# DeltaNet joins and pair weights apart from the recurrent steps, through DRAM, and gate products between the steps, in a two-layer hybrid encoder

## The chip, the cores and the metric

The kernel runs on one core of a Trainium2 chip. The metric is the device time of one execution in microseconds; each kernel is run several times and the median counts. One further execution is taken with the hardware profiler, and every row shown here comes from it.

TensorE (PE in the profile) multiplies matrices, VectorE (DVE), ScalarE (ACT) and GpSimd (POOL) work on tiles, and SyncE (SP) issues nearly all transfers of the part that the change touches. Each engine takes its instructions in one fixed order and waits at the first that isn't ready. Before the kernel is built, a scheduler writes these orders down, from the order of the program and its own estimates.

## The reference, cut to what matters

```python
# layer 0; DeltaNet runs once forwards and once on the flipped sequence
a = where(strict, beta * (k @ k.T) * gam, 0)          # gam = exp(gc_i - gc_j)
tmat = a + eye
u = solve_triangular(tmat, beta * v)
w = solve_triangular(tmat, beta * exp(gc) * k)
attn = (q @ k.T) * gam
def step(state, ...):                                 # over chunks of 64
    v_new = u - w @ state
    o = (q * exp(gc)) @ state + attn @ v_new
    state = exp(gl) * state + (k * exp(gl - gc)).T @ v_new
...
mix = concat([sigmoid(mo) * head_rms(mlstm), head_rms(deltanet)]) * silu(z)
x = x + gate * (mix @ w_out)
```

There are 1024 tokens, 1024 features, four mLSTM heads and four DeltaNet heads. A second layer (convolution and windowed attention) follows; the change doesn't touch it.

## The kernel before

The program treats the sequence in `NCH` = 8 chunks of 128 tokens, so that a triangular inverse of 128 by 128 per chunk, head and direction stands for two of the reference's chunks. Products of large matrices are made in three passes of 512 columns each: high part times high part, high times low, low times high (`whi`, `wlo` for weights, `hhi`, `hlo` for the normed input). ACT makes the high part of a weight (L264) and POOL the low part (L265).

Layer 0 goes through these stages. Projections of q, k and v for DeltaNet and mLSTM go on in the order of a list of steps (L925). `dn_system` builds the triangular systems per chunk and stores them to `nd_d` and `nt_d`. `dn_inverse` inverts blocks of 32, then joins them to blocks of 64, stored to `xl_d`; its last stages use the tiles `iG`, `iV`, `iT`. `mlstm` runs eight steps in both directions at once (`S`, `num`, `Cps`). `dn_step(j)` then runs the DeltaNet recurrence: chunk j forwards and chunk 7-j backwards. Last come the gates (`gate_chunk`, `gate_pair`), the output product and the second layer.

A `dn_step` of one direction loads the two 64-blocks of the inverse into `Y` (L951), loads two more blocks into `aux` (L953, L954), multiplies them (`T1`), copies the result (L958), multiplies again (`T2`) and copies it into `Y` (L962). This is the join of two blocks of 64. If the chunk is visited for the first time, it makes the pair weights of both directions: `KQ` on PE, two broadcast loads of `gc_d` (L975), a triangular mask (POOL, L599), four exponentials (ACT, L624), a product (DVE, L977); the other direction's weights go to `at_d` (L979) and are loaded at the second visit (L967). Then follow, in both cases, `kS` (from step 1 on), `Yr`, `qS`, `dS` (state update) and `o`, with ACT and DVE work after each.

`gate_chunk(c)` loads a weight of 512 KB (`wraw`, L258), splits it, multiplies (`z`) and applies the gate activation (L758 to L760), for c below 4 also `mo` (L768, L769); the result goes to `mix_d`. `gate_pair(6)` does two at once. `mix0(t)` loads the gates of 128 tokens (L1091), normalizes, transposes (`nT`) and multiplies (L1100). `out0(t)` splits that (L1054 on ACT, L1055 on DVE) and makes the output product `y`. In the program, `gate_chunk(2)` to `gate_chunk(5)` and `gate_pair(6)` stand behind all eight steps, and the scheduler mixes them in among these: `gate_pair(6)` is tied to the end of step 3, `mix0(3)`, the output weight and the first three `out0` to the end of `gate_pair`.

While layer 0 runs, SP also carries the loads of the second layer's modulation weight (L439), one `U` tile at a time, each made free by POOL (L443).

Of the kernel before, what the change touches and what calls it, by code (L numbers as in the profile page):

```python
# [17 lines left out]
P = 128  # L18
# [38 lines left out]
def trunk(ctx, tc, x, c, norm_g, ada_w, ada_b, ev_w_in, ev_m_gate_b, ev_dn_dt_bias, ev_dn_a_log,  # L57
# [69 lines left out]
    def nm(s):  # L127
        uid[0] += 1
        return f"{s}_{uid[0]}"
# [430 lines left out]
    nc.sync.dma_start(out=gc_d, in_=cs1[96:104])  # L560
    nc.sync.dma_start(out=nmu_d, in_=nmu[0:8])
# [40 lines left out]
    def brow(src, d, ch):  # L602
        return src[4 * d:4 * d + 4, ch * P:(ch + 1) * P].rearrange("(o h) l -> o h l", o=1).to_broadcast([P, 4, P])
# [32 lines left out]
    def dn_system(ch):  # L636
# [5 lines left out]
        nc.sync.dma_start(out=B_, in_=gc_d[:, tcs].rearrange("(o r) l -> o r l", o=1).to_broadcast([P, 8, P]))  # L642
# [15 lines left out]
    def dn_inverse(n):  # L658
# [41 lines left out]
        zd_r = ring(4096, 2, 4, 4, 32)  # L700
        own = diag4.rearrange("p (o g i) -> p o g i", o=1, g=4).to_broadcast([P, 4, 4, 32])
        spread = lambda ap: ap.rearrange("p u (o i) -> p u o i", o=1).to_broadcast([P, 4, 4, 32])
        for ch in range(NCH):
            u4 = slice(4 * ch, 4 * ch + 4)
            ZD, GD = next(zd_r), next(zd_r)
            nc.vector.tensor_tensor(out=ZD, in0=spread(Z[:, u4, :]), in1=own, op=ALU.mult)
            ps = bank(nm("iG"), (P, 4, 32), "C")
            for h in range(4):
                mm(ps[:, h, :], ZD[:, h].rearrange("p g i -> p (g i)"), AT[:, 4 * ch + h, :], True, True)
            nc.vector.tensor_tensor(out=GD, in0=spread(ps), in1=own, op=ALU.mult)  # L710
            ps = bank(nm("iV"), (P, 4, 32), "C")
            for h in range(4):
                mm(ps[:, h, :], GD[:, h].rearrange("p g i -> p (g i)"), B[:, 4 * ch + h, :], True, True)
            nc.scalar.copy(out=Z[:, u4, :], in_=ps)
            ps = bank(nm("iT"), (P, 4, 32), "C")
            tr(ps.rearrange("p g j -> p (g j)"), Z[:, u4, :].rearrange("p h i -> p (h i)"))
            nc.scalar.copy(out=VT[:, :, ch, :], in_=ps)
        for d, b, g_ in lanes4:
            nc.sync.dma_start(out=part(xl_d[0], d, b, 0, 1), in_=Z[g_])
        for h in range(4):  # L720
            nc.sync.dma_start(out=xl_d[1][:, :, :, h, 32:64, 0:32].rearrange("d b c i j -> i (d b c) j"),
                              in_=VT[32 * h:32 * h + 32].rearrange("p g c j -> p (g c) j"))

# [201 lines left out]
    for step, n in ((dn_q, 0), (dn_v, 0), (m_q, 0), (dn_q, 1), (m_q, 1), (dn_q, 2), (dn_q, 3), (m_k, 1), (m_v, 0), (m_v, 2), (m_v, 3), (m_v, 1), (m_k, 0), (mlstm, 0), (dn_v, 1), (dn_inverse, 0), (gate_chunk, 0), (dn_v, 2), (gate_chunk, 1), (dn_v, 3)):  # L925
        step(n)
    Y_r, aux_r, ke_r, vv_r, v2_r = (ring(0, 2, 4, P), ring(1024, 2, 2, 4, 64), ring(2048, 2, 4, P), ring(3072, 3, 4, P),
                                    ring(5632, 2, 4, P))
# [9 lines left out]
    seen2 = set()  # L938

    def dn_step(j):  # L940
        for d in range(2):
# [14 lines left out]
            for h in range(4):  # L956
                mm(ps[sb, h, :], aux[fb, 1, h, :], aux[fb, 0, h, :], True, True)
            nc.scalar.copy(out=aux[sb, 0], in_=ps[sb])  # L958
            ps = bank(nm("T2"), (P, 4, 64), "C")
            for h in range(4):  # L960
                mm(ps[fb, h, :], aux[sb, 0, h, :], Y[sb, h, sb], True, True)
            nc.scalar.copy(out=Y[fb, :, sb], in_=ps[fb])  # L962


            if ch in seen2:
                B_ = etile(("E", "Em")[d])
                nc.sync.dma_start(out=B_, in_=at_d[d, ch])  # L967
            else:
                ps = bank(nm("KQ"), (P, 4, P), "t")
                for h in range(4):  # L970
                    mm(ps[:, h, :], kT[h][:, tcs], qT[h][:, tcs], True, True)
                Bs = {}
                for d_ in (d, 1 - d):
                    B_ = Bs[d_] = etile(("E", "Em")[d_])
                    nc.sync.dma_start(out=B_, in_=brow(gc_d, d_, ch))  # L975
                    decays(B_, d_, ch)
                    nc.vector.tensor_tensor(out=B_, in0=B_, in1=ps, op=ALU.mult)  # L977
                B_ = Bs[d]
                nc.sync.dma_start(out=at_d[1 - d, ch], in_=Bs[1 - d])  # L979
# [167 lines left out]
    marks = [dn_step(j) for j in range(NCH)]  # L1147
    G2 = (None,)*4
    for cidx, j in zip(range(2, 6), G2):
        with ExitStack() if j is None else tc.issue_after(marks[j]):  # L1150
            gate_chunk(cidx)

    with tc.issue_after(marks[3]):
        half_done = gate_pair(6)
# [451 lines left out]
```

## Time and profile before

| | us |
|---|---|
| runs of the kernel | 1512.96, 1513.93, 1521.6 |
| their median | 1513.93 |
| the profiled execution | 1522.57 |
| span of its trace | 1520.8 |
| PE busy in the span | 1344.9 (88%) |
| DVE, ACT, POOL busy | 879.0, 585.9, 460.4 |

The profiled execution is 8.64 us longer than the median, and its mean granted TensorE clock is 0.933 of full speed. DeltaNet's steps lie between 549 us (the last mLSTM step) and 776 us (the first output product). From 866 us on only the second layer is left.

### The profile page before, as it was taken

How to read it: one execution, taken by the hardware profiler on the slowest of the kernel's cores; microseconds unless marked ns; L12 is line 12 of the kernel's file. 1: busy time of each engine (PE TensorE's matmuls, PEld its weight loads, DVE VectorE, ACT ScalarE, POOL GpSimd, SP SyncE). 2: the span in 40 equal slices, each digit the busy share in tenths (PEclk: the TensorE clock that was granted, in tenths of full speed). 3: DMA queues.
4: the chain of work that ended last, by engine and by line, in shares of the span. 5: the costliest groups of instructions: out<-in, count | busy, mean ns of one | idle time of the engine just before them, and what ended most of it. 6: DMA issues, size and time to landing. Idle time of an engine off the chain costs nothing. (4 is left out here: it accounts for less than half of the span.)

```text
span 1520.8 us, 20504 instructions
## 1 busy us (share of the span) xinstructions
PE 1344.9 (88%) x7331; PEld 1070.9 (70%) x7331; DVE 879.0 (58%) x1622; ACT 585.9 (39%) x1415; POOL 460.4 (30%) x357
## 2 busy tenths in 40 slices
PE   3978958878878988988999989889999999998998
PEld 2766746657667866777878857667776767876786
DVE  6789456933324641345854539998886454336334
ACT  5354454454444323343443321123324743326212
POOL 3454523444234511210234102322125233022210
PEclk9898987989899999889999999999999998997899
DMA  9334479369667785455655271010241233245322
GB/s 319 102 83 113 106 168 235 109 223 177 177 180 229 234 203 147 124 140 143 211 189 156 84 144 56 28 56 22 67 140 43 66 127 119 84 143 158 102 82 104
DMA packets 256456, 205.11 MB, mean 135 GB/s; under 512 B 59391, under 2 KB 219667, under 8 KB 256227
## 3 DMA queue, kind: packets, MB, share of 16 engines
q1 hardware_dynamic: 235555, 193.32, 45.1%
q10 hardware_dynamic: 20800, 10.49, 2.4%
q8 instruction: 58, 0.95, 0.3%
q14 instruction: 43, 0.35, 0.1%
HBM read 148.45 MB, written 58.98 MB: 136 GB/s over the span
## 5 line engine op out<-in xcount | busy, mean ns | idle before, releaser
L265 POOL TENSOR_TENSOR wlo<-wraw,whi 128x1024 fp32r<-128x1024 f32 x60 | 163.2, 2720 | 358.6 <-ACT whi L264 345.9
L1245 DVE SCALAR_TENSOR_TENSOR u<-xp,U,u 128x1009 f32<-128x1009 f32 (+14 forms) x120 | 176.2, 1502 | 1.0
L264 ACT CAST whi<-wraw 128x1024 fp32r<-128x1024 f32 x60 | 62.6, 1044 | 136.5 <-PE gb L139 49.1
L139 PE MATMUL z<-hhi,whi 128*128 128x512 f32 x256 | 108.1, 422 | 4.5 <-ACT mo L768 4.2
L139 PE MATMUL z<-hlo,whi 128*128 128x512 f32 x256 | 106.8, 417 | 0.0
L139 PE MATMUL z<-hhi,wlo 128*128 128x512 f32 x256 | 106.3, 415 | 0.0
L443 POOL TENSOR_TENSOR U<-U 128x512 f32<-128x512 f32 x56 | 79.4, 1419 | 76.9 <-ACT U L441 74.4
L139 PE MATMUL y<-wohi,mhi 128*128 128x512 f32 x240 | 97.9, 409 | 2.2 <-ACT mhi L1054 2.1
L139 PE MATMUL y<-wolo,mhi 128*128 128x512 f32 x240 | 96.8, 403 | 0.0
L139 PE MATMUL y<-wohi,mlo 128*128 128x512 f32 x240 | 96.1, 402 | 0.4 <-DVE mlo L1055 0.3
L441 ACT ACTIVATE U<-U,cs 128x512 f32<-128x512 f32 x64 | 45.9, 722 | 84.8 <-DMA U<-in_ada_w_dram 83.5
L599 POOL TENSOR_SCALAR_AFFINE_SELECT E<-E 128x512 f32<-128x512 f32 x32 | 21.4, 670 | 170.3 <-DMA E<-gc_d 71.3
L1397 DVE COPY U<-pT 128x512 f32<-128x512 f32 x48 | 32.5, 689 | 55.7 <-PE pT L158 55.6
L139 PEld LDWEIGHTS z<-hhi,whi 128*128 128x128 f32 x256 | 50.7, 198 | 16.7 <-ACT mo L768 4.6
L139 PEld LDWEIGHTS z<-hhi,wlo 128*128 128x128 f32 x256 | 50.5, 197 | 11.9 <-issue 1.1
L139 PEld LDWEIGHTS z<-hlo,whi 128*128 128x128 f32 x256 | 50.6, 197 | 11.3 <-issue 0.9
L139 PEld LDWEIGHTS y<-wohi,mhi 128*128 128x128 f32 x240 | 46.0, 192 | 13.5 <-ACT mhi L1054 2.5
L139 PE MATMUL sc<-ak,aq 128*128 128x256 f32 (+1 forms) x128 | 44.2, 429 | 11.6 <-DVE o L1372 9.8
L139 PEld LDWEIGHTS y<-wohi,mlo 128*128 128x128 f32 x240 | 45.9, 191 | 11.9 <-DVE mlo L1055 1.3
L1370 DVE CUSTOM_DVE_ANT_0 pt<-sc,U 128x256 f32<-128x256 f32 (+1 forms) x64 | 25.9, 404 | 48.6 <-PE sc L139 23.4
L139 PEld LDWEIGHTS y<-wolo,mhi 128*128 128x128 f32 x240 | 46.2, 193 | 10.3
L1374 ACT ACTIVATE pt<-pt,o 128x256 f32<-128x256 f32 (+1 forms) x64 | 31.4, 490 | 53.6 <-DVE o L1370 48.1
(455 smaller groups left out, 3603.7 us busy)
## 6 DMA issues: line engine op xcount, KB each, us to landing
wraw<-in_ev_w_in_dram SPq DMA_DIRECT2D x32, 512.0 KB
U<-in_ada_w_dram SPq DMA_DIRECT2D x64, 256.0 KB
wraw<-in_od_w_in_dram ACTq DMA_DIRECT2D x20, 512.0 KB
x<-in_x_dram SPq DMA_DIRECT2D x11, 512.0 KB
ada<-in_ada_w_dram SPq DMA_DIRECT2D x10, 512.0 KB
od_d<-o SPq DMA_DIRECT2D x64, 66.0 KB
U<-od_d SPq DMA_DIRECT2D x4, 1056.0 KB
U<-gc_d SPq DMA_DIRECT2D x8, 512.0 KB
```

The lines of the kernel that those rows point to most:

```text
L139: return nc.tensor.matmul(o, lhsT=l, rhs=r, start=s, stop=e, skip_group_check=shared).ins
L264: nc.scalar.copy(out=hi, in_=raw)
L265: nc.gpsimd.tensor_tensor(out=lo, in0=raw, in1=f(hi), op=ALU.subtract)
L441: nc.scalar.mul(out=t_ if k else acc, in_=t_, mul=cs[:, k:k + 1])
L443: nc.gpsimd.tensor_tensor(out=acc, in0=acc, in1=t_, op=ALU.add)
L599: nc.gpsimd.affine_select(out=ap, in_=ap, pattern=[[0, 4], [pat, P]], compare_op=ALU.is_ge, fill=NEG, base=0, channel_multiplier=cm_)
L1245: nc.vector.scalar_tensor_tensor(out=y[:, lo:hi], in0=xp[:, lo + d:hi + d], scalar=w_, in1=y[:, lo:hi], op0=ALU.mult, op1=ALU.add)
L1370: nc.vector.tensor_tensor_reduce(out=x1_, in0=ps[:, c0:c1], in1=bias[:, e, c0:c1], scale=1.0, scalar=1e30, op0=ALU.add, op1=ALU.min, accum ...
L1374: nc.scalar.activation(out=x1_, in_=x1_, func=AF.Exp, scale=-1.0, bias=mn1, accum_out=o2[:, 0, 128 + e:129 + e])
L1397: nc.vector.tensor_copy(out=PT, in_=tb)
```

## The change

The vectors `gc_d` and `nmu_d` are laid out by chunk, so that a broadcast load takes one run of 4 KB or 2 KB per partition in place of pieces of 512 bytes. The last stages of `dn_inverse` take two chunks at a time, with half as many instructions on ACT, and `dn_inverse` stands ahead of `mlstm` in the list of steps.

A new step `dn_joins` makes all joins ahead of the steps, two chunks and both directions together, and stores them to `xj_d` (per pair of chunks twelve loads of 64 KB, two products of 16 matmuls, two copies, two stores). `dn_weights(ch)` makes the pair weights of both directions of a chunk and stores both to `at_d`. In each step one direction now loads `Y` in three pieces and the pair weights from `at_d`. The ring of `Y` goes from two buffers to four, the ring of `aux` is gone.

Four of the eight `dn_weights` stand ahead of the steps, two ahead of step 0 and two ahead of step 1. The gates are written between the steps: `gate_chunk(2+j)` behind step j, `gate_pair(6)`, `mix0(3)` and the output weight behind step 4, `out0(3)` and `out0(4)` behind steps 5 and 6, and `out0(2)` behind the last.

The PE work is the same: 256 `T` records, the same `KQ`, `z`, `mo` and `y`. SP issues 47 transfers more.

```diff
-    nmu_d = dr.tile([8, T], F32, name="nmu_d")
+    nmu_d = dr.tile([NCH, 8, P], F32, name="nmu_d")
-    gc_d = dr.tile([8, T], F32, name="gc_d")
+    gc_d = dr.tile([NCH, 8, P], F32, name="gc_d")
...
     def brow(src, d, ch):
-        return src[4 * d:4 * d + 4, ch * P:(ch + 1) * P].rearrange("(o h) l -> o h l", o=1).to_broadcast([P, 4, P])
+        return src[ch:ch + 1, 4 * d:4 * d + 4, :].to_broadcast([P, 4, P])
...
-        nc.sync.dma_start(out=B_, in_=gc_d[:, tcs].rearrange("(o r) l -> o r l", o=1).to_broadcast([P, 8, P]))
+        nc.sync.dma_start(out=B_, in_=gc_d[ch:ch + 1].to_broadcast([P, 8, P]))
...
-        for ch in range(NCH):
-            u4 = slice(4 * ch, 4 * ch + 4)
...
+        for ch in range(0, NCH, 2):
+            u8 = slice(4 * ch, 4 * ch + 8)
...
+    def dn_joins(visits):
+
+
+        for chs in visits:
+            J = next(join_r)
+            G, N, C_, D_, R = [J[:, i].rearrange("p c (h i) -> p c h i", h=4) for i in range(5)]
...
+            for i, ch in enumerate(chs):
+                for d, (fb, sb) in enumerate(sides):
+                    for t_, src in ((G[fb, i], xl_d[1 - d][d, d, ch]), (N[fb, i], nd_d[d, ch, :, fb, sb]),
+                                    (D_[sb, i], xl_d[d][d, 1 - d, ch])):
+                        nc.sync.dma_start(out=t_, in_=src.rearrange("h j i -> j h i"))
+            for l, r, o, opens in ((N, G, C_, 0), (C_, D_, R, 1)):
+                ps = bank(nm("T"), (P, 2, 4, 64), "C")
...
+                nc.scalar.copy(out=o, in_=ps)
+            for i, ch in enumerate(chs):
+                nc.sync.dma_start(out=xj_d[ch].rearrange("d j h i -> (d j) h i"), in_=R[:, i])
...
-    for step, n in ((dn_q, 0), (dn_v, 0), (m_q, 0), (dn_q, 1), (m_q, 1), (dn_q, 2), (dn_q, 3), (m_k, 1), (m_v, 0), (m_v, 2), (m_v, 3), (m_v, 1), (m_k, 0), (mlstm, 0), (dn_v, 1), (dn_inverse, 0), (gate_chunk, 0), (dn_v, 2), (gate_chunk, 1), (dn_v, 3)):
+    for step, n in ((dn_q, 0), (dn_v, 0), (m_q, 0), (dn_q, 1), (m_q, 1), (dn_q, 2), (dn_q, 3), (m_k, 1), (m_v, 0), (m_v, 2), (m_v, 3), (m_v, 1), (m_k, 0), (dn_inverse, 0), (mlstm, 0), (dn_v, 1), (gate_chunk, 0), (dn_v, 2), (dn_v, 3), (dn_joins, ((0, 7), (1, 6), (2, 5), (3, 4))), (gate_chunk, 1)):
...
+    def dn_weights(ch):
+
+        tcs = slice(ch * P, ch * P + P)
+        ps = bank(nm("KQ"), (P, 4, P), "C")
+        for h in range(4):
+            mm(ps[:, h, :], kT[h][:, tcs], qT[h][:, tcs], True, True)
+        for d in range(2):
+            B_ = etile("Em")
+            nc.sync.dma_start(out=B_, in_=brow(gc_d, d, ch))
+            decays(B_, d, ch)
+            nc.vector.tensor_tensor(out=B_, in0=B_, in1=ps, op=ALU.mult)
+            nc.sync.dma_start(out=at_d[d, ch], in_=B_)
...
-            aux = next(aux_r)
-            nc.sync.dma_start(out=aux[fb, 0], in_=xl_d[1 - d][d, d, ch].rearrange("h j i -> j h i"))
-            nc.sync.dma_start(out=aux[fb, 1], in_=nd_d[d, ch, :, fb, sb].rearrange("h j i -> j h i"))
-            ps = bank(nm("T1"), (P, 4, 64), "C")
...
+            nc.sync.dma_start(out=Y[fb, :, sb], in_=xj_d[ch, d])
+            B_ = etile("E")
+            nc.sync.dma_start(out=B_, in_=at_d[d, ch])
...
-    marks = [dn_step(j) for j in range(NCH)]
...
+    visits = [0, 7, 1, 6, 2, 5, 3, 4]
+    for ch in visits[0:4]:
+        dn_weights(ch)
+
+
+    for j in range(NCH):
+        for ch in visits[2 * j + 4:2 * j + 6]:
+            dn_weights(ch)
+        dn_step(j)
+        if j < 4:
+            gate_chunk(2 + j)
+        elif j == 4:
+            gate_pair(6)
...
+            mixed.append(mix0(3, True))
+            wo = load_wout(ev_w_out[0], g0)
+        elif j < 7:
+            out0(*((3, None, (4,)), (4, None, (2,)))[j - 5])
+    out0(2, None, (1,))
```

On PE, before, the last mLSTM numerators are followed by the first `KQ` and a long row of gate products `mo` (of `gate_chunk`).

```order
L139 MATMUL num_3299<-U 128x129
L158 MATMUL iT_3650<-ident,U 128x128
L139 MATMUL KQ_4176<-qT_4139,kT_656 128x128
L139 MATMUL KQ_4176<-qT_4141,kT_657 128x128
L139 MATMUL KQ_4176<-qT_4143,kT_658 128x128
L139 MATMUL KQ_4176<-qT_4145,kT_659 128x128
L139 MATMUL mo_5384<-hhi_35_236,whi_5379 128x512
```

On PE, now, the same place holds the last joins (`T`), two `KQ`, and work of the first step, up to the first gate product `z` of `gate_chunk(2)`.

```order
L139 MATMUL num_3502<-U 128x129
L139 MATMUL T_4091<-U 64x64 x12
L139 MATMUL mo_4284<-hlo_48_249,whi_4226 128x512
...
L139 MATMUL T_4123<-U 64x64 x16
L139 MATMUL T_4141<-U 64x64 x16
...
L139 MATMUL Yr_4531<-U 128x128 x4
L139 MATMUL dS_4512<-U 128x128 x4
L139 MATMUL kS_4743<-U,kT_656 128x128
...
L139 MATMUL qS_4763<-U,qT_4318 128x128
L139 MATMUL z_4564<-hhi_35_236,whi_4556 128x512
```

The gate products that stood behind the last numerators have moved ahead of them in part; 14 of `mo` are left, and behind them the joins, and then the first step, stand before `z`.

On SP, before, at this place, one first broadcast load of `gc_d` is followed by loads of the step (`E` is the tile of pair weights) and, some rows on, the next gate weight (`wraw`).

```order
L982 DMA U_75<-vt_d_661 128x512
L975 DMA E_500_4181<-gc_d_1013 128x4x128
L999 DMA U_75<-kt_d_660 128x512
L719 DMA xl0_d_1072<-U_75 32x32x32 x4
L418 DMA vt_d_661<-vt_496_4136 128x4x128
L975 DMA E_509_4258<-gc_d_1013 128x4x128
```

On SP, now, the loads of the first two pair weights, the steps' loads, their store to `at_d`, and loads for the second layer (L439, `in_ada_w_dram`) stand ahead of the two gate weights `wraw`.

```order
L974 DMA E_495_4348<-gc_d_1013 128x512
L990 DMA U_75<-xl0_d_1072 64x4x64 x2
...
L439 DMA U_75<-in_ada_w_dram 128x512
L996 DMA U_75<-vt_d_661 128x512
L977 DMA at_d_4324<-E_494_4337 128x512
L1013 DMA U_75<-kt_d_660 128x512
L439 DMA U_75<-in_ada_w_dram 128x512
L258 DMA wraw_520_4555<-in_ev_w_in_dram 128x8x128
L977 DMA at_d_4324<-E_495_4348 128x512
L258 DMA wraw_526_4621<-in_ev_w_in_dram 128x8x128
```

The gate weight of `gate_chunk(2)` has moved behind the store of the first pair weights on the queue.

On PE, before, the last steps are followed by the transposes (`nT`) of `mix0` and the first output product `y`.

```order
L139 MATMUL o_5301<-U,E_5275 128x128 x3
L158 MATMUL nT_5856<-ident,E_5854 128x128 x4
L158 MATMUL nT_5952<-ident,E_5950 128x128 x4
L139 MATMUL gps_5444<-U,one 1x512
L158 MATMUL nT_5960<-ident,E_5958 128x128 x4
L139 MATMUL y_5966<-wohi_5866,mhi_5928 128x512
```

On PE, now, the last product of `gate_pair(6)` (`z`) is followed by one step's products and `nT`, and then by `y`, with work of the last steps behind.

```order
L139 MATMUL z_5502<-hhi_46_247,wlo_5411 128x512
L139 MATMUL kS_5638<-U,kT_657 128x128
...
L139 MATMUL Yr_5647<-U 128x128 x4
...
L158 MATMUL nT_5553<-ident,E_5551 128x128 x4
L158 MATMUL nT_5561<-ident,E_5559 128x128 x4
L139 MATMUL Yr_5698<-U 128x128 x4
L139 MATMUL dS_5663<-U 128x128 x4
L139 MATMUL o_5672<-U,E_5635 128x128 x4
L139 MATMUL kS_5839<-U,kT_656 128x128
L139 MATMUL y_5773<-wohi_5571,mhi_5735 128x512
```

The first `y` has moved from behind the last step to 36 matmuls behind the last `z`.

## Rows read from the trace of the kernel before

**Rows 1.** Windows by stage: start:end, length, busy us (records) by engine, PEclk, DMA, GB/s.

```profile
351.00:470.00 119.00, 97.54 (x487) 77.69 (x485) 48.14 (x85) 49.86 (x120) 48.07 (x41) 0.89 0.68 185
549.00:704.00 155.00, 131.35 (x782) 112.03 (x779) 49.89 (x127) 58.91 (x168) 27.67 (x33) 0.88 0.56 141
704.00:776.00 72.00, 68.71 (x499) 59.44 (x498) 53.87 (x139) 31.94 (x89) 16.31 (x14) 1.00 0.71 222
```

**Rows 2.** What PE waited for, 549 to 704 us: total us, times, longest.

```profile
PE T L139 <- DMA U<-xl_d: 8.5, 2, 4.5
PE Yr L139 <- ACT U L962: 5.4, 2, 4.7
PE z L139 <- ACT mo L768: 4.2, 1, 4.2
PE T L139 <- DMA U<-nd_d: 3.2, 1, 3.2
PE T L139 <- ACT U L958: 2.2, 1, 2.2
```

**Rows 3.** Windows by tile, 549 to 704 us: z (PE, PEld, DVE, ACT), mo, T (PE, PEld, ACT).

```profile
549.00:704.00 155.00, 40.82 (x146) 29.89 (x147) 4.12 (x6) 3.54 (x6) 0.88 0.56 141
549.00:704.00 155.00, 22.97 (x93) 17.21 (x93) 4.42 (x4) 2.38 (x4) 0.88 0.56 141
549.00:704.00 155.00, 16.90 (x168) 13.33 (x168) 7.70 (x21) 0.88 0.56 141
```

**Rows 4.** Timeline of PE around 750 us: start, length, instruction.

```profile
747.99 1.06 PE L139 MATMUL Yr<-U 128*128 128x128 f32 x8
748.97 0.44 PE L139 MATMUL T<-U 64*64 64x64 f32 x4
749.34 0.50 PE L139 MATMUL z<-hhi,wlo 128*128 128x512 f32 x1
749.91 0.39 PE L139 MATMUL z<-hlo,whi 128*128 128x512 f32 x1
750.14 0.40 PE L139 MATMUL z<-hhi,wlo 128*128 128x512 f32 x1
```

**Rows 5.** Timeline of SP, DVE and POOL behind the last mLSTM numerators.

```profile
548.49 0.39 SPq L975 DMA_DIRECT2D E<-gc_d  x1
549.94 1.12 DVE L862 SCALAR_TENSOR_TENSOR E<-num,den,E 128x128 f32<-128x128 f32 x4
553.79 0.63 POOL L599 TENSOR_SCALAR_AFFINE_SELECT E<-E 128x512 f32<-128x512 f32 x1 [8.63 <-DMA xl_d<-U]
554.39 2.41 POOL L265 TENSOR_TENSOR wlo<-wraw,whi 128x1024 fp32r<-128x1024 f32 x1
555.83 0.69 DVE L977 TENSOR_TENSOR E<-E,KQ 128x512 f32<-128x512 f32 x1 [4.64 <-issue]
```

**Rows 6.** Groups of ACT by line, 549 to 776 us: busy, mean ns, idle before.

```profile
L264 ACT CAST whi<-wraw 128x1024 fp32r<-128x1024 f32 x5 | 5.2, 1039 | 1.8 <-PE z L139 1.8
```

**Rows 7.** What SP's queue waited for, 549 to 704 us; the last row is 320 to 800 us.

```profile
SPq L951 <- PE T L139: 21.2, 3, 7.6
SPq L975 <- DMA at_d<-E: 10.7, 4, 4.5
...
SPq L439 <- POOL U L443: 34.5, 19, 6.3
```

**Rows 8.** Timeline of SP, DVE and PE between the last gate product and the first output product.

```profile
755.97 0.32 SPq L788 DMA_DIRECT2D mix_d<-zt  x1
761.35 0.38 SPq L1091 DMA_DIRECT2D g<-mix_d  x1
770.67 0.69 DVE L1100 TENSOR_TENSOR g<-nT,g 128x512 f32<-128x512 f32 x1 [1.91 <-PE nT L158]
775.83 1.23 DVE L1055 TENSOR_TENSOR mlo<-g,mhi 128x1024 fp32r<-128x1024 f32 x1
775.85 0.50 PE L139 MATMUL y<-wohi,mhi 128*128 128x512 f32 x1 [0.79 <-ACT mhi L1054]
```

**Rows 9.** Timeline of SP and POOL in dn_system: a load and the mask that waits for it.

```profile
197.71 2.29 SPq L642 DMA_DIRECT2D U<-gc_d  x2
207.18 1.22 POOL L599 TENSOR_SCALAR_AFFINE_SELECT U<-U 128x512 f32<-128x512 f32 x2 [15.01 <-DMA U<-gc_d]
```

More of the change, by code (lines that the diff above doesn't have):

```diff
@@ L699, in dn_inverse @@
         VT = sl(3072, 4, 8, 32)
-        zd_r = ring(4096, 2, 4, 4, 32)
-        own = diag4.rearrange("p (o g i) -> p o g i", o=1, g=4).to_broadcast([P, 4, 4, 32])
-        spread = lambda ap: ap.rearrange("p u (o i) -> p u o i", o=1).to_broadcast([P, 4, 4, 32])
-        for ch in range(NCH):
-            u4 = slice(4 * ch, 4 * ch + 4)
[L705 to L717, printed above, removed]
+        ZD = sl(4096, 8, P)
@@ new lines, in dn_inverse @@
+        ZD = ZD.rearrange("p u (g i) -> p u g i", g=4)
+        own = diag4.rearrange("p (o g i) -> p o g i", o=1, g=4).to_broadcast([P, 8, 4, 32])
+        spread = lambda ap: ap.rearrange("p u (o i) -> p u o i", o=1).to_broadcast([P, 8, 4, 32])
+        for ch in range(0, NCH, 2):
+            u8 = slice(4 * ch, 4 * ch + 8)
+            nc.vector.tensor_tensor(out=ZD, in0=spread(Z[:, u8, :]), in1=own, op=ALU.mult)
+            ps = bank(nm("iG"), (P, 8, 32), "C")
+            for u in range(8):
+                mm(ps[:, u, :], ZD[:, u].rearrange("p g i -> p (g i)"), AT[:, 4 * ch + u, :], True, True)
+            nc.vector.tensor_tensor(out=ZD, in0=spread(ps), in1=own, op=ALU.mult)
+            ps = bank(nm("iV"), (P, 8, 32), "C")
+            for u in range(8):
+                mm(ps[:, u, :], ZD[:, u].rearrange("p g i -> p (g i)"), B[:, 4 * ch + u, :], True, True)
+            nc.scalar.copy(out=Z[:, u8, :], in_=ps)
+            ps = bank(nm("iT"), (P, 2, 4, 32), "C")
+            for i in range(2):
+                tr(ps[:, i].rearrange("p g j -> p (g j)"), Z[:, 4 * ch + 4 * i:4 * ch + 4 * i + 4, :].rearrange("p h i -> p (h i)"))
+            nc.scalar.copy(out=VT[:, :, ch:ch + 2, :], in_=ps.rearrange("p c g j -> p g c j"))
@@ L1146, in trunk @@
     wo = None
-    marks = [dn_step(j) for j in range(NCH)]
[L1148 to L1154, printed above, removed]
-    assert next(pace["gen"], None) is None and pace.get("done")
-    with tc.issue_after(half_done):
-        g0 = [sl(7424 + 512 * i, 512) for i in range(2)]
-        for i in range(2):
-            nc.sync.dma_start(out=g0[i], in_=g_row[0:1, half(i)].to_broadcast([P, 512]))
-        mixed.append(mix0(3, True))
-        wo = load_wout(ev_w_out[0], g0)
-        for ti, after in ((3, (4,)), (4, (2,)), (2, (1,))):
-            out0(ti, None, after)
+    visits = [0, 7, 1, 6, 2, 5, 3, 4]
[9 more added lines that the diff above has]
+            gate_pair(6)
+            assert next(pace["gen"], None) is None and pace.get("done")
+            g0 = [sl(7424 + 512 * i, 512) for i in range(2)]
+            for i in range(2):
+                nc.sync.dma_start(out=g0[i], in_=g_row[0:1, half(i)].to_broadcast([P, 512]))
+            mixed.append(mix0(3, True))
[3 more added lines that the diff above has]
+    out0(2, None, (1,))
     fold(1, 0, 8)
```

37 lines of the change are left out of this document (11 added, 26 removed).

## The prediction

> **What bounds the kernel now.** I read the windows by stage first, since PE is busy 88% of the span and a gain has to be a stretch where it isn't. In the DeltaNet steps up to the last gate products (549 to 704 us) PE is busy 131.35 of 155 us, and its granted clock has a mean of 0.88; from 704 to 776 us, where the same steps go on, it is busy 68.71 of 72 us at 1.00 [rows 1]. So the first of the two windows has something to win and the second almost nothing. Then I read what PE waited for in it: of 23.65 us idle, 11.7 us is `T` waiting for loads of `xl_d` and `nd_d`, 2.2 us `T` for ACT's copy of the first join product, 5.4 us `Yr` for the second copy, and 4.2 us is `z` waiting for a gate activation [rows 2]. All but the last belong to the joins inside the steps. The mLSTM window (351 to 470 us) idles 21.46 us too, but its waits are in the loop of `S` and `num`, whose instructions the change leaves as they are.
>
> How much of the first window is lost in all? PE has 782 records there: 146 of `z` and 93 of `mo` with 512 columns, 168 of `T`, and 375 others, nearly all of 128 columns [rows 1, 3]. At the full clock, shown by the stretch around 750 us, records start 0.23 us apart with 512 columns, (748.97 - 747.99) / 8 = 0.1225 us apart for `Yr`, and (749.34 - 748.97) / 4 = 0.0925 us apart for `T` [rows 4]. That is 239 x 0.233 = 55.7, 375 x 0.1225 = 45.9 and 168 x 0.0925 = 15.5, together 117 us of work in 155 us. **38 us is lost**: 23.65 us idle and some 14 us in which PE runs at the lower of its two clock levels after it idled. This is the most that the change can take from this stage.
>
> **What is removed.** The waits of `T` and `Yr` go with the joins that leave the steps: 19.3 us idle by their rows. Their work does not go, since the 256 records of `T` stay, only batched. ACT loses half its small copies (16 of each kind become eight in all), which costs PE nothing at either end. In the steps SP no longer waits for `T` before it can issue the next `Y` load, 21.2 us of waiting over three times [rows 7]; that was hidden where the next rows of its queue were not yet due, so I count it within the 38 us and not again. The low-clock share goes if the idle that causes it goes.
>
> **What is added.** Joins: per pair of chunks 12 loads, 2 stores and 32 matmuls of `T`. They stand beside `dn_v` and `mo`, 512-column products that need none of their results, so I cost their own waits at nothing; without that cover one join round costs what the step's did, 19.3 us over 14 step halves, or 1.4 us each. Pair weights: eight visits with two broadcast loads each. Rows of before price the chain: the load is issued at 548.49, POOL's mask starts at 553.79 (5.3 us later), and DVE's product ends at 555.83 + 0.69 = 556.52, so **8.0 us** from issue to weight [rows 5]. With a store of up to 5.3 us, a visit's two tiles turn over in some 12 us, against 8 to 19 us of PE work between two `KQ` in the new order. In the middle of the steps this fits, and I charge 4 us for the gate wait that stays [rows 2] and 3 us for DVE.
>
> **The start of the steps.** Here a new wait arises, seen in SP's order: the first pair's store and several L439 loads stand ahead of the weight of `gate_chunk(2)`, and SP waits at each. Count from the last numerators (N). DVE's products of the mLSTM output take eight times 0.28 us plus what lies between them, estimated N + 4; their store frees the tile at N + 7.5 (estimate, below the 5.3 us of a load); the pair weight takes 8.0 us more, N + 15.5 [rows 5]. Two L439 loads wait 34.5 / 19 = 1.8 us each on the mean, N + 19 [rows 7]. The weight's load, at the 5.3 us of the pair weight as the nearest row, N + 24.5; ACT's high part 1.04 us [rows 6] and POOL's low part 2.41 us [rows 5], N + 28; with a store that the queue waits for, N + 30. PE has until then 14 `mo` (3.3 us), 44 matmuls of `T` at two records each (8.1 us) and 28 of 128 columns (6.9 us), together 18.3 us. So PE idles about 12 us, bounds 0 (if the store doesn't hold the queue) and 18, plus about 5 us at the lower clock, in the proportion 14 to 24 of before. **17 us**.
>
> The Trainium skill (DMA: Bandwidth & Descriptors, section "Anatomy of one DMA — SWDGE (gpsimd) path") puts a transfer at about 2 us fixed plus bytes over 436 GB/s, 2.6 us for 256 KB. By that figure this term would be some 8 us smaller. The trace does not agree: 5.3 us at this place [rows 5].
>
> **The end of the steps.** `out0(3)` now comes 36 matmuls behind the last `z`, 8.4 us of work, where before all the last steps lay between: the last `z` ended at 750.54, the store of its gate was issued at 755.97, the load of gates at 761.35, the first multiplication started at 770.67, and `y` at 775.85 after 0.79 us idle [rows 4, 8]. The chain that must now fit in 8.4 us: activation 2 to 5.4 us, store landing 4 to 5.4, load 4 to 5.3, two multiplications of 0.69, `mhi` and `mlo` 1.04 and 1.23; 13.7 to 19.8 us [rows 6, 8]. Wait 5 to 11 us; I take 7, near the lower end, since behind `gate_pair` the queue is emptier, and 3 us of lower clock. **10 us**. The last steps behind `y` are then covered by its work, but DeltaNet's own 0.8 us idle there was all there was to win.
>
> **Broadcast loads.** The eight loads of `gc_d` in `dn_system` get larger pieces. One mask waited 15.01 us for a pair of them [rows 9], although in that stretch stores of `nd_d` share the queue. Bounds: 0 and -6 us; I take -2, since SP issues those stores in between and they do not change. Moving `dn_inverse` ahead of `mlstm` gives and takes cover in the mLSTM window: -5 to +8, 0 taken. SP's 47 extra transfers cost it 0.3 to 0.6 us each to issue [rows 5, 8], some 20 us on an engine that has room, hidden unless they stand ahead of a late load (that is the third rival).
>
> **The sum.** -38 (all that is lost) + 17 (start) + 10 (end) + 4 + 3 (middle) = -4; -2 for the broadcasts; **-6 us**. Against the profiled execution of 1522.57 us, 1516.6 us. That execution was 8.6 us longer than the median, in the way of run to run, so the change is applied to the median: 1513.93 - 6 = **1508 us**.
>
> **Rivals.** First, the waits at both ends are covered: the store does not hold the queue at the start and the gate chain takes its lower bounds. Then 7 us in the middle and 3 elsewhere remain of 38, a gain of 28: **1486 us**. For it speaks that 19.3 us of waits really go; against it, that the queue's rows stand as they stand. It decides if `z` starts within 20 us of the last numerators.
>
> Second, the transfers on the start's chain land in about half of 5.3 us, because broadcast pieces are larger: three transfers by 2.7 us, 8 us, and 2 of clock, **1498 us**. No row of before shows such a load landing sooner. The figure of the Trainium skill (DMA: Bandwidth & Descriptors, the same section) for such a transfer lies near this.
>
> Third, slower: SP's queue holds back not just the first gate weight but those of all four `gate_chunk`s and both of `gate_pair(6)`, each behind two pair-weight stores or L439 loads. At up to 6.3 us for one L439 wait and 10.7 / 4 = 2.7 us for a wait on `at_d` [rows 7], 6 us each is 36 us: **1544 us**. It decides from 3.5 us each, 21 us, which puts the time past 1529. For it speaks that the queue is one and in order, with 47 entries more; against it, that the queue's own waits in this stretch on `T`, 21.2 us, go [rows 7].
>
> That the change doesn't do what it says is small: PE's order shows the joins batched ahead of the steps and `y` beside them.
>
> **How the numbers follow.** A measurement of this kernel can hardly tell a change within 1% from none, which is 1498.8 to 1529.1 us. Chances: waits change place (1508) 0.39; covered ends (1486) 0.28; faster landings (1498) 0.08; queue (1544) 0.25. Faster by over 1%: 0.28 + 0.08 = 0.36; slower 0.25; same 0.39. The range leaves out a tenth at either end: below, the covered case less the 6 us of the broadcasts, 1480; above, up to the middle between the deciding point and the queue's price, 1537.
>
> **What the profile after would show.** If I am right, `T` no longer waits for `xl_d` inside the steps, `z` of the first gate in the steps waits about 12 us for its weight or ACT, `y` waits 5 to 11 us for a gate load or `mhi`, and the mLSTM window keeps its length within 8 us. If the first rival holds, the window of the steps loses some 28 us and its clock rises to 0.95 or more. If the third holds, POOL and PE wait on `wraw` in five or six places, and SP's waits on L977 stores and on L439 add up to over 40 us. A first output product before the last step's `o` shows that the end was overlapped at all; if `y` stands there and PE still idles, DVE is late. I am wrong if the projections or `dn_system` change by more than 8 us, which no row here prices.

## The result, and the profile after

The changed kernel takes 1473.18 us (median of 4 runs, 1472.01 to 1474.99) against 1513.88 us: ratio 0.9723, interval 0.9694 to 0.9752, so 40.7 us less. The forecast was 1508 us, the range 1480 to 1537.

First the windows of the changed kernel by stage, from the first mLSTM product `S` to the last numerators, on to the first output product `y`, and on to the second layer's first transposes; columns as in [rows 1].

```profile
334.20:519.60 185.40, 162.23 (x1111) 131.21 (x1112) 82.55 (x203) 66.91 (x160) 63.83 (x71) 0.93 0.72 207
519.60:717.00 197.40, 167.04 (x986) 143.30 (x987) 91.37 (x203) 88.04 (x225) 58.84 (x54) 0.91 0.71 211
717.00:808.40 91.40, 90.79 (x500) 76.95 (x500) 50.90 (x119) 31.94 (x113) 26.54 (x26) 0.99 0.47 154
```

PE still idles 30.4 us in the steps. That is a little more than before, where [rows 1] have 23.65 and 3.29 us in a longer stretch. So waits did change place. What PE waited for from 519 to 717 us, to be held against [rows 2]:

```profile
PE KQ L139 <- DVE E L976: 9.2, 3, 4.7
PE Yr L139 <- DMA U<-vt_d: 5.2, 1, 5.2
PE KQ L139 <- ACT U L747: 3.9, 1, 3.9
PE Yr L139 <- DVE U L1002: 2.9, 2, 2.0
...
PE KQ L139 <- DMA qT<-qT_d: 1.8, 1, 1.8
...
PE z L139 <- POOL wlo L265: 1.2, 1, 1.2
```

`T` no longer waits for `xl_d`; `KQ` waits instead, for the product of the chunk before (L976), which holds its bank. Most of the gain lies ahead of all this. The instructions of tile `S`, of the kernel before and of the changed one (count, shortest/median/longest in ns, first and last start in us):

```profile
L139 PE MATMUL S<-mq,mk x64: 272/284/579, 350.8 to 453.5; 64*128 64x128 f32 x64
```

```profile
L139 PE MATMUL S<-mq,mk x64: 271/272/547, 334.2 to 420.4; 64*128 64x128 f32 x64
```

`S` begins 16.6 us sooner, and its stage is shorter by another 13.5 us (198.9 to 185.4). In `dn_system`, POOL's masks that waited for a load of `gc_d` in five places, one of them in [rows 9], 28.3 us in all, wait in one:

```profile
198.56 1.22 POOL L599 TENSOR_SCALAR_AFFINE_SELECT U<-U 128x512 f32<-128x512 f32 x2 [9.61 <-DMA U<-gc_d]
```

From the last numerators to the second layer's transposes it is 288.8 us after 297.1. The second layer, which the change leaves alone, takes 674.0 us in the profiled execution of before and 664.8 us in that of the changed kernel; profiles of the kernels below, which all leave it alone too, have 658.3 to 677.9 us there. So the last 9 us of the difference between the spans (47.6 us) can't be put down to the change. In these traces SP issues 769 transfers after 713, so 56 more, and not 47.

### The profile page after: what moved, and what is told of

It is laid out like the page before. It is cut to its first block, busy times and chain, and to the rows that moved or that the text cites. A ratio compares the mean times of both kernels' runs of the same rounds, so it can differ in the third digit from the quotient of the medians.

```text
span 1473.2 us, 20504 instructions
## 1 busy us (share of the span) xinstructions
PE 1316.9 (89%) x7331; PEld 1054.8 (72%) x7331; DVE 878.4 (60%) x1614; ACT 578.2 (39%) x1383; POOL 467.5 (32%) x357
## 4 chain that ended last, share of the span: by engine, by line
PE 52%; DVE 17%; DMA 15%; issue 5%; ACT 4%; SPq 3%; POOL 2%; POOLq 0%; DVEq 0%; ACTq 0%
PE y L139 11%; PE z L139 10%; DVE u L1264 5%; PE sc L139 4%; PE ob L139 2%; PE aq L139 2%; PE pT L158 2%; PE av L139 2%; PE ak L139 2%; PE dq L139 2%; DMA E<-nmu_d 2%; PE mq L139 2%; DVE U L683 2%; DMA E<-gc_d 2%; DVE U L212 1%
```

## The experiments

Theory A: the layout of the broadcast vectors made the gain, through loads that land sooner, and the rest of the change gives little. Rival B: the gain comes from the moved work, and the layout is worth the 2 us of the forecast. Medians are of 4 runs (of 10 where rows lie 4096 bytes apart in rooms of their own, e14), beside 7 to 13 of the kernel before on the same chip (1512.89 to 1514.83 us); ratios are to that, with the 95% interval.

**Layout alone, and all but the layout.** Two edits on the kernel before; and the reverse on the changed kernel.

```diff
-    gc_d = dr.tile([8, T], F32, name="gc_d")
+    gc_d = dr.tile([NCH, 8, P], F32, name="gc_d")
     (nmu_d, the stores and brow likewise)
```

> The kernel before with nothing but the new layout of gc_d and nmu_d. Theory A (the stage ahead of the first mLSTM product S became 16.6 us shorter because the broadcast loads land sooner): 14 to 20 us less than the kernel before, that is some 1494 to 1500 us, and S starts near 334 us; the pair-weight loads in the steps and the nmu loads in the mLSTM stage may add a few us. Theory B (the stage became shorter because the list of steps and the scheduler's order changed): within 6 us of the kernel before, S near 350 us.

Measured: 1460.75 us, 0.9653 (0.9623 to 0.9684), 52 us less than before and 12 less than the whole change. The order of instructions on PE, DVE, ACT and POOL is the same as before (and, by the names in the trace, on SP), so nothing but the transfers of the two vectors can have done it. Theory A's size, 14 to 20 us, was far too small.

> The changed kernel with the old layout of gc_d and nmu_d (pieces of 512 bytes). Theory A: 14 to 25 us more than the changed kernel, S near 350 us. Theory B: within 6 us of the changed kernel. If the layout also carries the pair weights in the steps, the loss there shows as a longer stretch between the last mLSTM numerators and the first output product.

Measured: 1527.6 us, 1.0096 (1.0066 to 1.0127). **All the rest of the change costs 15 us without the layout.** Theory A holds and B falls, but A's size (54 us here where 14 to 25 were expected) and its "little" were wrong too. By the trace, the stage of `S` is 200.1 us long and the rest of layer 0 307.3 us, against 198.9 and 297.1 before the change: the moved work costs its time behind the last numerators. From these to the first output product it takes 216.0 us, against 197.4 with the layout, so the layout carries the pair weights too.

The traces show how. With the layout alone `S` starts at 333.3 us (350.8 before), its stage takes 177.8 us (198.9), and the rest of layer 0 278.7 us (297.1): 17.5, 21.1 and 18.4 us, so each stage gains. In the mLSTM stage, SP issues a load of `nmu_d` and POOL masks it. In the kernel before, the issues (SP), then the masks (POOL):

```profile
387.16 0.38 SPq L813 DMA_DIRECT2D E<-nmu_d  x1
392.77 0.36 SPq L813 DMA_DIRECT2D E<-nmu_d  x1
398.58 0.36 SPq L813 DMA_DIRECT2D E<-nmu_d  x1
405.24 0.37 SPq L813 DMA_DIRECT2D E<-nmu_d  x1
...
392.29 0.64 POOL L599 TENSOR_SCALAR_AFFINE_SELECT E<-E 128x512 f32<-128x512 f32 x1 [8.87 <-DMA E<-nmu_d]
397.71 0.63 POOL L599 TENSOR_SCALAR_AFFINE_SELECT E<-E 128x512 f32<-128x512 f32 x1 [4.78 <-DMA E<-nmu_d]
```

And with the layout alone:

```profile
364.70 0.33 SPq L813 DMA_DIRECT2D E<-nmu_d  x1
368.73 0.33 SPq L813 DMA_DIRECT2D E<-nmu_d  x1
373.58 0.33 SPq L813 DMA_DIRECT2D E<-nmu_d  x1
378.04 0.32 SPq L813 DMA_DIRECT2D E<-nmu_d  x1
...
368.29 0.64 POOL L599 TENSOR_SCALAR_AFFINE_SELECT E<-E 128x512 f32<-128x512 f32 x1 [7.19 <-DMA E<-nmu_d]
372.69 0.98 POOL L599 TENSOR_SCALAR_AFFINE_SELECT E<-E 128x512 f32<-128x512 f32 x1 [3.77 <-DMA E<-nmu_d]
```

From issue to mask it was 5.13 and 4.94 us and is 3.59 and 3.96. Loads follow each other in (405.24 - 387.16) / 3 = 6.03 us before and (378.04 - 364.70) / 3 = 4.45 us now, since the next issue comes when a tile is free, and that comes behind the mask. From the first to the last of the stage's 14 loads it is 101.3 us (357.38 to 458.68) before and 82.9 us (338.85 to 421.79) now: 18.4 of the 21.1 us that the stage gains.

**nmu_d alone.**

```diff
-    nmu_d = dr.tile([8, T], F32, name="nmu_d")
+    nmu_d = dr.tile([NCH, 8, P], F32, name="nmu_d")
     (gc_d as before)
```

> The kernel before with the new layout of nmu_d alone (the loads of the mLSTM stage), gc_d as it was. The layout of both took some 52 us off the kernel before, 17 ahead of the first S, 21 in the mLSTM stage and 18 in the steps by their traces. Theory A (each stage gains by its own loads, whose landing is on its chain): S stays near 350 us, the mLSTM stage shortens by 15 to 22 us, the steps don't change; 1490 to 1500 us. Theory B (512-byte pieces load the shared DMA queue, and every stage gains from the whole): the mLSTM stage gains less than 10 us, and others gain too.

Measured: 1494.3 us, 0.9858 (0.9828 to 0.9887). The mLSTM stage is 176.0 us long (345.8 to the last numerators at 521.7), 23 less. The rest of layer 0 is 300.0 us (297.1), and `S` comes 5 us sooner. Each stage gains by its own loads.

**Is it the pieces' size or their addresses?** Five kernels, all the kernel before with another room for the same rows.

```diff
+    gc_d = dr.tile([NCH, 8, P + 32], ...)       # 512-byte pieces, 640 bytes apart
+    gc_d = dr.tile([NCH, 4, 2 * P + 32], ...)   # 1 KB pieces, 1152 bytes apart
+    gc_d = dr.tile([8, T + 32], ...)            # 512-byte pieces, 4224 bytes apart
+    gc_d = dr.tile([NCH, 8, 1024], ...)         # 512-byte pieces, 4096 bytes apart
+    gc_d = dr.tile([NCH, 8, 512], ...)          # 512-byte pieces, 2048 bytes apart
     (one of these; nmu_d likewise)
```

> The kernel before with both vectors laid out by chunk, but each row of 512 bytes followed by 128 bytes of padding, so that a load takes pieces of 512 bytes again, from one small region. Theory A (the number of pieces, 512 or 1024 per load in place of 128, sets how late the load lands): the time of the kernel before, within 5 us of 1513. Theory B (the distance of 4 KB between the pieces was what cost): that of the layout alone, some 1460 us.

Measured: 1466.96 us, 0.9685 (0.9643 to 0.9726): nearly all the gain, with as many pieces as before. DMA packets of the kernel before, and of this one:

```profile
DMA packets 256456, 205.11 MB, mean 135 GB/s; under 512 B 59391, under 2 KB 219667, under 8 KB 256227
```

```profile
DMA packets 256568, 205.11 MB, mean 140 GB/s; under 512 B 59391, under 2 KB 219795, under 8 KB 256339
```

> The kernel before with two rows of both vectors side by side and 128 bytes of padding behind, so that a load takes pieces of 1 KB, half as many as before. If the time goes by the number of pieces: most of the gain of the layout alone (a step load has 256 pieces in place of 512, and would have 128): 1470 to 1490 us. If only the last step to one piece per partition counts: within 8 us of 1513.

Measured: 1463.81 us, 0.9667 (0.9624 to 0.9709); half the pieces of the one above, and no difference beyond the intervals. So neither the number nor the size of pieces is the cause. My theory A on pieces falls.

> The kernel before with both vectors still laid out by row, eight rows of 1024 numbers, but with 128 bytes of padding behind each row, so that the pieces of a broadcast load lie 4224 bytes apart in place of 4096. Nothing else differs, the order of instructions included. Theory A (what cost was that all pieces of a load lie a round power of two apart): 1460 to 1475 us, as with the padded rows of 512 bytes. Theory B (what cost was that the pieces lie far apart, whatever the number): within 5 us of the kernel before.

Measured: 1496.66 us, 0.9894 (0.9833 to 0.9956): 18 us of the 52, a third. The order of instructions is the same as before on all engines, SP included. Neither theory's number. By the traces `S` starts 12.5 us sooner (338.3 after 350.8 us), and its stage and the rest of layer 0 are only 6.5 and 6.3 us shorter.

> The kernel before with both vectors laid out by chunk as in the change, but each row of 512 bytes in a room of 4096 bytes. Theories A and B both expect the time of the kernel before, within 6 us, if the distance of 4096 bytes within one load is the cause. If it comes out near 1465 us, the cause lies in what neighbouring loads share in the layout by row (chunks side by side in one row), and not in the distance.

Measured: 1521.46 us, 1.0043 (1.0016 to 1.0069): the layout by chunk gains nothing if the rows lie 4096 bytes apart.

> As the layout with rooms of 4096 bytes, but rooms of 2048 bytes. Theory A (round distances): slow or partly slow, 1480 to 1513 us. Theory B (distance): about half the gain, 1485 to 1495 us. Near 1465 us: the limit lies between 2048 and 4096 bytes.

Measured: 1466.6 us, 0.9693 (0.9643 to 0.9742), the full gain. **The distance of 4096 bytes between a load's pieces is what cost.** The same load shows it, here the fifth of `gc_d` in the steps, in rooms of 4096 bytes, in rooms of 2048, and in rows 4224 bytes apart:

```profile
593.77 0.38 SPq L975 DMA_DIRECT2D E<-gc_d  x1
599.13 0.64 POOL L599 TENSOR_SCALAR_AFFINE_SELECT E<-E 128x512 f32<-128x512 f32 x1 [9.73 <-DMA E<-gc_d]
```

```profile
548.61 0.38 SPq L975 DMA_DIRECT2D E<-gc_d  x1
552.03 0.64 POOL L599 TENSOR_SCALAR_AFFINE_SELECT E<-E 128x512 f32<-128x512 f32 x1 [7.37 <-DMA E<-gc_d]
```

```profile
563.28 0.38 SPq L975 DMA_DIRECT2D E<-gc_d  x1
568.34 0.64 POOL L599 TENSOR_SCALAR_AFFINE_SELECT E<-E 128x512 f32<-128x512 f32 x1 [9.59 <-DMA E<-gc_d]
```

That is 5.36, 3.42 and 5.06 us from issue to mask. The mean over all loads of four pieces (`nmu_d`, and `gc_d` in the steps) whose mask waited for them:

| bytes from piece to piece | us from issue to mask, loads | time, us |
|---|---|---|
| 4096, by row (before) | 6.2, 20 | 1513 to 1515 |
| 4096, by chunk (e14) | 6.2, 22 | 1521.46 |
| 4224 (e13) | 5.9, 21 | 1496.66 |
| 2048 (e15) | 4.6, 22 | 1466.6 |
| 640 (e10) | 4.6, 18 | 1466.96 |
| 512, one run (e1) | 4.2, 17 | 1460.75 |

That the distance is round accounts for some of the time (4224 bytes: 18 us less), but not for all, since loads of four pieces land nearly as late at 4224, and 2048 is as round and costs nothing that can be measured. Whether it is the distance as such or the stretch of memory that one load touches (four pieces 4096 bytes apart, or 2048) stays open.

**The parts beside the layout.** All of these have the layout. Edits on the changed kernel: gates written behind the steps as before (e4); pair weights in the steps (e5); joins in the steps (e6); `dn_inverse` behind `mlstm` (e8); joins and pair weights both in the steps (e12). On the layout alone: gates by hand (e16); `dn_inverse` as changed (e17); gates by hand with the new order of the list (e18). The expectations follow in this order.

```diff
-        dn_weights(ch)                    # e4: gates behind, by the scheduler
+        marks.append(dn_step(j))
+    with tc.issue_after(marks[3]):
+        half_done = gate_pair(6)
...
-            nc.sync.dma_start(out=B_, in_=at_d[d, ch])          # e5: KQ, decays in dn_step again
-            nc.sync.dma_start(out=Y[fb, :, sb], in_=xj_d[ch, d])  # e6: aux, T1, T2 in dn_step again
-(dn_inverse, 0), (mlstm, 0), (dn_v, 1)    # e8: behind
+(mlstm, 0), (dn_v, 1), (dn_inverse, 0)
```

> The changed kernel with the gates, the output weight and the first three output products written behind all eight steps and left to the scheduler, as in the kernel before. Theory A (placing them by hand lets the last steps be covered by output products, and costs little at the start): 5 to 12 us slower than the changed kernel. Theory B (the scheduler's mixing was as good, the gain is all in joins, weights and layout): within 2 us.

> The changed kernel with the pair weights made in the steps again, as before, joins and gates as changed. If taking the pair weights out of the steps is worth something of its own: 4 to 12 us slower than the changed kernel, with PE waiting for o or KQ in the steps. If it only moves a wait (KQ now waits 9.2 us in three places for the product that frees its bank): within 3 us, or faster.

> The changed kernel with the joins in the steps again (the aux ring, two products, two copies per step and direction), pair weights and gates as changed. If the joins are the main part of the gain in the steps: 15 to 30 us slower (13 us of PE work of T back, and the waits of T and Yr). If the gain came from the gates and pair weights: under 8 us.

> The changed kernel with dn_inverse behind mlstm in the list of steps again. If its place ahead of the mLSTM steps costs or gives nothing by itself, as I had it: within 3 us. If it is what lets the joins end before the steps: 5 to 15 us slower, with PE idle between the last numerators and the first Yr.

> The changed kernel with joins and pair weights both in the steps again; what is left of the change is the layout, dn_inverse in pairs ahead of mlstm, and gates placed by hand. Undoing either alone gave 7 to 8 us. If their costs are separate, both give 12 to 18 us: 1457 to 1462 us, as fast as the layout alone or faster. If the hand-placed gates are worth anything beside the layout alone (1460.75 us), under 1456 us. If the two were in each other's way, 1464 us as each alone.

> The layout alone with the gates, output weight and first output products placed by hand between the steps, and nothing else of the change (dn_inverse as before, joins and pair weights in the steps). The version with dn_inverse changed as well took 1451.15 us, the layout alone 1460.75 us. If the placement gives these 10 us: 1449 to 1454 us. If dn_inverse gives them: 1458 to 1463 us.

> The layout with dn_inverse as changed (in pairs of chunks, ahead of mlstm in the list, gate_chunk(1) last), and gates left to the scheduler as before. Gates placed by hand beside the layout gave nothing (1464.72 against 1460.75 us), with dn_inverse changed as well 1451.15 us. If dn_inverse gives the 10 us by itself: 1449 to 1454 us. If only both together do: 1458 us or more.

> The layout, gates by hand and the changed order of the list of steps (dn_inverse ahead of mlstm), but dn_inverse chunk by chunk as before. If the order of the list gives the gain beside hand-placed gates: 1450 to 1455 us. If the pairs of chunks give it: 1460 to 1466 us.

| dn_inverse | gates | joins, pair weights | us | ratio, interval |
|---|---|---|---|---|
| before | scheduler | in steps, in steps (e1) | 1460.75 | 0.9653, 0.9623 to 0.9684 |
| before | by hand | in steps, in steps (e16) | 1464.72 | 0.968, 0.9631 to 0.973 |
| in pairs, ahead | scheduler | in steps, in steps (e17) | **1441.93** | 0.9535, 0.9489 to 0.9581 |
| by chunk, ahead | by hand | in steps, in steps (e18) | 1454.2 | 0.9603, 0.9564 to 0.9642 |
| in pairs, ahead | by hand | in steps, in steps (e12) | 1451.15 | 0.9577, 0.9554 to 0.96 |
| in pairs, ahead | by hand | apart, in steps (e5) | 1466.11 | 0.9671, 0.9636 to 0.9706 |
| in pairs, ahead | by hand | in steps, apart (e6) | 1464.84 | 0.9668, 0.9628 to 0.9707 |
| in pairs, behind | by hand | apart, apart (e8) | 1479.56 | 0.9757, 0.9713 to 0.9801 |
| in pairs, ahead | scheduler | apart, apart (e4) | 1494.44 | 0.9858, 0.9818 to 0.9899 |
| in pairs, ahead | by hand | apart, apart (the change) | 1473.18 | 0.9723, 0.9694 to 0.9752 |

Several of these expectations missed: e4 cost 21 us where 5 to 12 were expected, e6 was 8 us faster than the change where it should have been slower, and e17 came out 7 us below its fastest case; e12 fell under its 1456 us, but hand-placed gates are not why (e16). Joins and pair weights apart cost 14 to 15 us each, and 22 us together, against both in the steps. For the pair weights this price includes two things that the change moves with them: `KQ` shares the PSUM bank of the joins (before, that of `qS`), and the new weights use a ring of two tiles (before, two rings of two). Gates by hand are worth 21 us while both are apart, and cost 9 us by the medians while both are in the steps, which the intervals don't separate: with both apart and gates behind, one transpose waits long, as the waits of PE in that kernel (515 to 750 us) show:

```profile
PE nT L158 <- DVE g L1114: 16.2, 1, 16.2
PE o L139 <- DMA E<-at_d: 7.1, 6, 2.2
```

`dn_inverse` ahead of `mlstm` and in pairs takes 19 us off the layout alone and gives **the fastest kernel, 31 us below the changed one**. Beside gates by hand the order of the list carries most of it: 10.5 us from e16 to e18, whose intervals touch, and 3 more with pairs (e12), which the intervals don't separate. In the changed kernel itself, with gates by hand and joins and weights apart, putting `dn_inverse` behind again (e8) costs 6 us, which is not shown, since the intervals overlap. In the waits of PE in the steps, with the layout alone (511 to 718 us) and with `dn_inverse` as changed too (500 to 780 us), the wait for the blocks that it stores is gone:

```profile
PE T L139 <- DMA U<-xl_d: 6.6, 3, 3.1
PE z L139 <- ACT mo L768: 3.0, 1, 3.0
```

```profile
PE T L139 <- ACT U L963: 2.1, 1, 2.1
PE qS L139 <- DVE ogd L1030: 1.5, 1, 1.5
...
PE T L139 <- DMA U<-xl_d: 0.2, 1, 0.2
```

In the two profiles some 11 us of the gain lie between `S` and the second layer's transposes (456.5 to 445.7 us) and 6.5 us in the second layer, which varies as said above; so of the 19 us between the medians 11 are shown in the stages that the edit touches, and the rest is open.

**Joins by side.** The changed kernel with one side of the array after the other.

```diff
-                for i in range(2):
-                    for h in range(4):
-                        for fb, sb in sides:
+                for fb, sb in sides:
+                    for i in range(2):
+                        for h in range(4):
```

> The changed kernel, whose joins issue the eight matmuls of one side of the array and then the eight of the other, in place of alternating sides. Theory A (the joins' PE work itself shrank, from 24.7 us to 11.4 us, because matmuls on opposite quarters of the array overlap when they alternate): the busy time of T goes to 17 us or more, and the kernel is 3 to 8 us slower. Theory B (batching alone, fewer waits and restarts, shrank it): T stays under 13 us and the time within 1.5 us.

Measured: 1478.1 us, 0.9763 (0.9735 to 0.979). Windows of tile `T` (PE, PEld, ACT) in the changed kernel, and here:

```profile
440.00:530.00 90.00, 11.39 (x256) 9.10 (x256) 4.15 (x7) 0.91 0.69 199
```

```profile
440.00:530.00 90.00, 18.70 (x256) 16.52 (x256) 4.71 (x8) 0.92 0.73 212
```

In the kernel before, from 549 to 776 us, the same columns read:

```profile
549.00:776.00 227.00, 24.71 (x256) 19.39 (x256) 11.72 (x32) 0.92 0.61 167
```

Of the 13.3 us that the joins' work shrank by, 7.3 come from the alternation, as A says, and the other 6.0 come with the batching alone. The 4.9 us in time are not shown, since the two intervals overlap.

**KQ in two banks.** The wait of 9.2 us that the changed kernel shows.

```diff
-        ps = bank(nm("KQ"), (P, 4, P), "C")
+        ps = bank(nm("KQ"), (P, 4, P), "Ct"[visits.index(ch) % 2])
```

> The changed kernel with the KQ of every second chunk in the other single PSUM bank (the one of qS), so that two KQ can be under way. If KQ's three waits of 9.2 us for the product of the chunk before are what is left to win in the steps: 5 to 10 us faster than the changed kernel. If the wait is only moved, to the tile of the weights or to qS: within 2 us. If qS now waits for a KQ that waits for its loads: slower by 3 us or more.

Measured: 1475.88 us, 0.9732 (0.9688 to 0.9776). In its trace `KQ` waits for L976 only once, 1.9 us, but `Yr` still waits 5.3 us for `vt_d` and `nT` 4.3 us for POOL, and no difference in time is shown.

## Why the prediction was wrong

**Broadcast loads, -2 us (bounds 0 and -6).** This is the step that failed: measured alone, -52 us. I priced it from one wait of 15.01 us that shares its queue with stores [rows 9], and took the stores to be the cause since they do not change. They were not: with the layout alone, no mask in `dn_system` waits for `gc_d`. My own sign of being wrong came about: the stretch ahead of `S` changed by 16.6 us, where I allowed 8, and the mLSTM stage by 13.5. I left out the loads of `nmu_d` in the mLSTM stage, though the diff names that vector, because I had put that window's idle down to the loop of `S` and `num`: its waits end at DVE. The largest of them, in the kernel before (351 to 470 us) and with the layout alone (333 to 511 us):

```profile
PE S L139 <- DVE E L818: 10.5, 4, 2.9
```

```profile
PE S L139 <- DVE E L818: 0.3, 1, 0.3
```

Behind DVE stands a chain of which I read only the first link. In the kernel before, what DVE, ACT and POOL waited for from 351 to 450 us:

```profile
DVE E L818 <- ACT E L816: 11.0, 3, 5.6
```

```profile
ACT E L816 <- POOL E L599: 31.4, 9, 6.7
```

```profile
POOL E L599 <- DMA E<-nmu_d: 33.5, 7, 8.9
```

(For a further 27.3 us ahead of L818 the trace names nothing that DVE waited for.) And I did not carry the second rival's sooner landing beyond the start of the steps. That rival had the sooner landing that decided, though for another reason, and on one chain of three transfers in place of 40 loads in three stages, each on a chain that the next one waits for.

**Why the loads land sooner.** I had thought of piece size, and the runs show the addresses. The Trainium skill (DMA: Bandwidth & Descriptors, section "Latency and other measured facts") reports that large power-of-two pitches between rows in HBM slow transfers down to half the rate, that 4 KiB of padding restores it and 192 bytes do not, and calls the cause an inference. Its pitches are 512 KiB and more; here 4096 bytes cost and 2048 don't, and 128 bytes of padding gave back a third.

**All else, -4 us: measured +15 without the layout, +12 with it.** The sum began from 38 us lost in the steps, and took all of it as the change's to win. The joins' waits of [rows 2] were in part the late loads: with the layout alone, and joins where they were, `T` waits 6.6 us for `xl_d` and `Yr` 2.0 us for the second copy up to the first output product, where before it was 9.7 and 5.4 us (549 to 776 us). The sum has a slip besides: in the proportion that it names, 14 to 24, the lower clock at the two ends would be 7 and 4 us in place of 5 and 3, and the sum -1 in place of -4.

**The start of the steps, 12 us idle: right in size.** Five waits from 526 to 552 us add up to 3.90 + 1.77 + 5.19 + 0.87 + 1.25 = 13.0 us, and the first gate product starts at 549.08, 29.5 us behind the last numerators (forecast: 30). But PE stood at `KQ` and `Yr` for most of it, for a bank that the last join holds and for loads of `qT_d` and `vt_d`; `z` itself waits 1.25 us. The chain that I counted was there beside these waits and ended with them, with ACT's high part of the gate weight just ahead of `z`:

```profile
547.98 1.04 ACT L264 CAST whi<-wraw 128x1024 fp32r<-128x1024 f32 x1 [0.67 <-DMA wraw<-in_ev_w_in_dram]
```

The first rival, which needed `z` within 20 us, is out. The 5.3 us per load behind this forecast run from issue to a mask whose wait the trace ends with a store to `xl_d` [rows 5]; the next five loads whose masks did wait for them took 4.6 to 6.4 us, so the figure stands.

**The middle, 4 + 3 us: too small.** `KQ` alone waits 9.2 us in three places. All three, and the `KQ` ahead of the last, on PE's timeline:

```profile
578.68 1.13 PE L139 MATMUL KQ<-qT,kT 128*128 128x128 f32 x8 [0.44 <-DVE E L976]
...
590.82 2.04 PE L139 MATMUL KQ<-qT,kT 128*128 128x128 f32 x8 [4.12 <-DVE E L976]
...
613.33 1.05 PE L139 MATMUL KQ<-qT,kT 128*128 128x128 f32 x8
...
625.29 2.04 PE L139 MATMUL KQ<-qT,kT 128*128 128x128 f32 x8 [4.65 <-DVE E L976]
```

The last two long waits end 12.1 and 12.0 us behind the `KQ` ahead of them. So a visit of `dn_weights` takes about the 12 us that I gave it, and what failed is its cover: PE came to the next `KQ` after 8.0 and 7.3 us, at the lower end of my 8 to 19. SP's queue waits there too; its longest waits from 334 to 800 us begin with the store that must land before the next weight can be loaded into its tile, 23.5 us in ten places, against 10.7 in four before [rows 7]:

```profile
SPq L974 <- DMA at_d<-E: 23.5, 10, 4.3
...
SPq L439 <- POOL U L443: 8.5, 7, 3.9
```

The wait that the third rival rested on, L439, fell from 34.5 to 9.3 us (320 to 800 us); that rival did not come about. Without the layout the time, 1527.6 us, comes near that rival's deciding point, but not by its mechanism: there too PE waits only 1.2 us for a gate weight (`z` for POOL's low part).

**The end, 7 us idle: right in size, by luck.** From 698 to 716 us the trace has five waits of 1.01, 2.00, 1.47, 0.93 and 1.78 us, 7.2 us, at `qS`, `Yr`, `nT`, `Yr` and `dS`, and `y` waits for nothing. The priced chain of gate load, `mhi` and `mlo` held up nothing at `y`; most of the waits are the steps' own.

**"Their work does not go."** It did in part: the 256 records of `T` take 11.39 us in place of 24.71, and the joins by side (e3) show why for 7.3 of these 13.3 us.

The range left out the result because its lower end rested on these bounds of the broadcast term. Its forecast for the other parts, a gain of 4 us, had the wrong sign as well.

## What to carry to other kernels

When a change alters the layout of a tensor, list every load of it in every stage and ask which of them sits on a chain that the next load waits for; a wait that the trace puts down to an engine may end at a load some links back. Change one thing at a time: here a layout of six lines gave more than the whole change, and the larger parts beside it, taken together, cost 12 us. Before moving work through DRAM out of a loop, count the tiles and banks through which it must pass: a store that has to land before its tile is loaded again can pace the moved loop. (Here the queue waited 23.5 us for such stores; no run shows how much of the 14 us for the pair weights is theirs, and a second bank for `KQ` gave nothing that is shown.)

## What the runs showed of the hardware that was not expected

A broadcast load of four 512-byte pieces reached its mask 6.2 us behind its issue, on the mean, with the pieces 4096 bytes apart, 5.9 us at 4224, 4.6 us at 2048 and at 640, and 4.2 us when they were side by side. In time that was 1513 to 1521 us at 4096 bytes, 1497 at 4224, 1467 at 2048 and at 640, and 1461 at 512, with the same order of instructions by the names in the traces and, but for the last (237113 packets), nearly equal packets (256456 to 256568). Matmuls of 64 by 64 that alternate between two opposite quarters of the array took 11.39 us of PE for 256 records, and 18.70 us when the eight of one quarter came first.
